# One decoder layer on one core: the first 512 channels projected together, in four banks, while x arrives

## The chip, the core and the metric

The kernel runs on one core of one Trainium2 chip. The metric is the device time of one execution in microseconds (us). The engines are named as the profile names them: PE is the matrix engine (PEld its weight loads), ACT the scalar engine, DVE the vector engine, POOL the general one, and SP the one that issues DMAs.

## What is computed

One layer of a decoder for 256 tokens of 1024 channels, all in float32: a combined projection of x, three branches that read it (block attention, a short convolution, dilated attention), their gated sum, an output projection and a layer norm, and then a gated feed-forward part with a convolution and a second layer norm. Cut to what matters:

```python
qa, ka, va, qd, kd, vd, b_gate, c_gate, hc, gate_logits = split(x @ w_in)   # x: 256 x 1024
y_moba = moba_attention(qa, ka, va)                    # 8 heads of 64
y_conv = b_gate * causal_dwconv(c_gate * hc, w_short_conv)
y_dil  = dilated_mixture(qd, kd, vd)                   # 12 heads of 64, 3 groups
g = sigmoid(gate_logits)
x = LN(alpha * x + (g0 * (y_moba @ w_moba_proj) + g1 * (y_conv @ w_conv_proj)
                    + g2 * (y_dil @ w_dil_proj)) @ w_mix_out)
u = causal_dwconv(x @ w_up, w_ffn_conv) + b_ffn_conv
x = LN(alpha * x + (silu(u_gate) * u_val) @ w_down)
```

## The kernel before, in words

All weights pass through SBUF once, as a stream of blocks of 1 MB: 1024 rows of a weight matrix by 256 columns. `load_next` (line 111) issues the DMA of a block on SP's queue into one of three `raw` buffers. `prep` (line 129) cuts a block into four pieces of 512 columns of the buffer and splits each into two float32r parts: ACT copies the piece rounded (`split`, line 149), DVE subtracts to get the remainder (line 150). Whoever splits the last piece of a block issues the load of the third next block. `LEAD = 10` bounds how many pieces may be split and not yet used.

A product of two split operands takes three matmuls, high by high, high by low and low by high. `project` (line 209) makes two tiles of 128 channels by 256 tokens: 48 matmuls of 256 columns, in one PSUM bank of the pool `acc` (three banks) for each tile. After each tile `tick` (line 155) splits the next pieces and runs the tile's consumer. For the queries of the dilated attention the consumer (`queries`, line 233) is two copies of 64 partitions by 256 columns on ACT (line 239), each followed by a subtraction on DVE (line 240).

The start differs from the steady course. Seven bf16 matmuls on zeros (`WARM`, line 172) stand first on PE. x comes in four quarters of 256 columns (256 KB), each followed on SP's queue by a quarter of the first weight block, then a quarter each of the second block, then the third block whole. PE transposes each quarter of x (four transposes, line 194) and ACT and DVE split it. `first_products` (line 94) makes the first two tiles of queries quarter by quarter: 12 matmuls (line 439) for each quarter, 48 in all. From line 112 on `project` makes the other tiles. In the tables below a "product" is one of these matmuls of 256 columns.

The order on each engine is fixed when the program is built: every engine takes its instructions strictly in its own list's order, and waits on semaphores for the others. Two rows of the layer norm's gain and offset (`gB`, `bB`, line 115) and small convolution weights (`small_loads`, line 411) are loaded on SP's queue too; the small weights are transposed on PE (lines 423 and 425).

Of the kernel before, what the change touches and what calls it, by code (L numbers as in the profile page):

```python
# [14 lines left out]
P = 128  # L15
# [18 lines left out]
WARM = 7  # L34
# [3 lines left out]
def trunk(ctx: ExitStack, tc, x, w_in, w_short_conv, w_moba_proj, w_dil_proj, w_conv_proj, w_mix_out,  # L38
# [27 lines left out]
    # ---- the stream of weights: blocks of up to [128, 2048] are loaded, and in pieces of 512 columns  # L66
    # ---- rounded to the tensor engine's 12-bit form, with the remainder
    blocks = []

    def block(*parts):  # L70
        """parts: DRAM access patterns [128, k, columns], one behind the other in the block"""
        blocks.append(parts)
# [10 lines left out]
    columns(DIL_Q, 3)  # L83
# [27 lines left out]
    def load_next(between=None):  # L111
# [5 lines left out]
        for p in blocks[i]:  # L117
            k, c = p.shape[1:]
            step = 2 if i < 2 else k
            for k0 in range(0, k, step):  # L120
                if between:
                    between(k0 // step)
                n = step * c
                nc.sync.dma_start(r[:, at:at + n].rearrange("p (k c) -> p k c", c=c), p[:, k0:k0 + step, :])  # L124
                at += n
# [3 lines left out]
    def prep(n=1):  # L129
        """the next n pieces, as far as they may run ahead"""  # L130
# [11 lines left out]
    def take(n):  # L142
        """the next n pieces"""
        i = used[0]
        assert len(ready) >= i + n, (len(ready), i, n)
        return ready[i:i + n]
# [5 lines left out]
    # ---- work set between the products that hold the tensor engine  # L152
    side, late = [], []

    def tick(n, consume=None, ahead=1):
        """after n pieces' worth of products: what the last time left, more weights, what takes these
        products, and a stage of the work that is set between"""
# [9 lines left out]
    # ---- the tensor engine's clock is raised while the first loads are under way  # L167
# [6 lines left out]
    # ---- x, and its transpose  # L174
    xs = act.tile([P, 2, D], F32, tag="xs", name="xs", bufs=2)
    xv = x.rearrange("(t p) c -> p t c", p=P)
    load_next(lambda c: nc.sync.dma_start(xs[:, :, c * 256:c * 256 + 256], xv[:, :, c * 256:c * 256 + 256]))  # L177
    for i in range(1, RAW):
        load_next()
# [17 lines left out]
    # ---- products  # L197
    def mm3(o, ah, al, bh, bl, first, last):
        """o += (ah + al)' (bh + bl), all but the product of the two remainders (2^-24)"""
# [4 lines left out]
    def cut(w, k, c0, c1):  # L204
        """rows k, columns c0..c1 of a block of 256 columns in pieces w"""
# [3 lines left out]
    def project(consume, xh=xTh, xl=xTl, ahead=1):  # L209
        """[128 channels, 256 tokens] for two tiles of channels; consume(tile, product)"""  # L210
# [7 lines left out]
    def project_tokens():  # L218
        """tokens by 256 channels, in two parts: [128 tokens, 2, 256 channels]"""
# [10 lines left out]
    # ---- attention: heads go in pairs, head a of a pair at partitions 64 a  # L230
    HALF = (slice(0, 64), slice(64, 128))

    def queries(store):
        """per tile of two heads: [part and remainder of a head, 2 heads, 256 tokens]"""
# [9 lines left out]
    def keys(store):  # L244
        """per tile: the part of a head, twice [128, 2 heads, 256 tokens]; the remainders [128, 256]"""
# [15 lines left out]
    def scores(o, q, k, a, t):  # L261
        """o [128 queries of tile t, 256 keys] for head a of a pair"""
# [5 lines left out]
    def exponentials(e, parts):  # L268
        """parts: (part of e, scores in PSUM, mask); e = exp((s + mask) / 8 - max); returns its sums"""
# [12 lines left out]
    def turned(blks):  # L282
        """transposes of up to four [128, 128] tiles, split: two of [128, 4, 128]"""
# [12 lines left out]
    def values(vs, ps, c):  # L296
        """vs: per group (vh, vl); ps: per group the transposed probabilities of keys 0..127 and 128..255"""
# [14 lines left out]
    def dilated(c, dq, dk, dv, y):  # L312
        """the stages of a pair of heads, the three groups in one softmax"""
# [75 lines left out]
    # ---- masks (additive), by shape alone  # L389
# [14 lines left out]
    # ---- small per-channel weights, turned to columns  # L404
# [24 lines left out]
    # ---- the mixer's projections and attention  # L429
    dq, dk, dv = [[], [], []], [[], [], []], []  # L430
    o = [acc((P, T)) for _ in range(2)]

    def first_products(k2):
        w = ready[k2]
        for xt, i in ((xTh, 0), (xTl, 0), (xTh, 1)):
            for k in (2 * k2, 2 * k2 + 1):
                for c in range(2):
                    s = (k % 2) * 256 + c * P
                    nc.tensor.matmul(o[c], w[i][:, s:s + P], xt[:, k, :], start=k + i == 0 and xt is xTh,  # L439
                                     stop=k == KT - 1 and i == 1)  # L440

    for k2 in range(KT // 2):
        transpose_x(k2)
        prep()
# [3 lines left out]
    q = queries(dq[0])  # L448
    for c in range(2):
        tick(2, lambda: q(c, o[c]), 1)  # L450
    for g in range(1, 3):
        project(queries(dq[g]), ahead=0)
    small_loads()
    gB, bB = rows(ln1_g, "gB"), rows(ln1_b, "bB")
# [48 lines left out]
    # ---- gates and branch projections  # L503
# [27 lines left out]
    # ---- layer norm  # L531
# [3 lines left out]
    def residual(r, res, o, st, i, c0, c1):  # L535
        """columns c0..c1 of r = ALPHA res + o, with their statistics"""
# [3 lines left out]
    def norm(r, st, gB, bB, ends, done=lambda c0, c1: None):  # L540
        """over r, in parts of columns that end at ends; done(first column, last)"""
# [12 lines left out]
    def row_products(o, a, w, k, t, c0, c1, first, last):  # L554
        """o += columns c0..c1 of row k of a block of 1024 columns, in pieces w, by the tokens of tile t"""
# [4 lines left out]
    def sums():  # L560
        """banks of the sums of the two token tiles by parts of the columns: (first column, last, sum)"""
# [5 lines left out]
    def finish(o, t, parts, r, res, between=lambda: None):  # L567
        """the last products of token tile t, in parts of columns that end one after the other, and the
        residual sum; parts: (activations, pieces of the weights)"""
# [14 lines left out]
    # ---- output projection of the mixer, tokens by channels  # L584
# [39 lines left out]
    # ---- gated feed-forward with a causal convolution  # L624
# [6 lines left out]
    def hidden(j):  # L631
        """the consumers of the two halves of w_up, and what they give"""
# [99 lines left out]
```

## Time and profile before

| | |
|---|---|
| times of three executions | 495.58, 497.87, 500.51 us, median 497.87 |
| span of the profiled execution, first to last instruction | 493.7 us |
| its own time | not given apart from its span; the span is 1.9 us under the shortest and 4.2 under the median of the three times |
| PE / PEld / DVE / ACT busy | 98% / 93% / 73% / 55% of the span |
| DMA | 83.51 MB, mean 169 GB/s |
| mean granted clock of PE | 0.991 |

The profile names a group of instructions by line, engine, operation and tiles (out<-in), with its busy time. A row of the timeline has start, length, engine, line, operation, tiles, shape and count; in brackets stands the idle time of the engine before it, and what ended it. A merged row's length runs from the first start to the last end; a matmul's own length is longer than the spacing to the next, since they are pipelined.

### The profile page before, as it was taken

The page shows a single profiled execution, that of the slowest core. Times are in us where ns is not written, and L with a number is a line of the kernel's source. Part 1 is how long each engine was busy: PE and PEld are TensorE (multiplying, and loading weights), DVE is VectorE, ACT ScalarE, POOL GpSimd, SP SyncE. Part 2 cuts the span into 40 slices and gives each one's busy share as a digit, 9 for nine tenths or more (in the row PEclk, how much of TensorE's full clock was granted, in tenths as well). Part 3 has the DMA queues.
Part 4 walks back from the last instruction along what each step waited for, and adds up shares of the span by engine and source line. Part 5 has one row for each costly group of instructions (what it writes and reads, how often), then busy time and mean ns, then how long its engine had stood idle before and what let it go on. Part 6 is the DMA issues. An engine that isn't in the chain of part 4 may idle for free.

```text
span 493.7 us, 9076 instructions
## 1 busy us (share of the span) xinstructions
PE 483.7 (98%) x3582; PEld 457.3 (93%) x3582; DVE 361.6 (73%) x775; ACT 271.9 (55%) x579; POOL 4.3 (1%) x9
## 2 busy tenths in 40 slices
PE   8999999999999999999999999999999999999993
PEld 5999788999899999999999889999999999999983
DVE  6888768476788865656565986798677867776966
ACT  4768455364756673535353712876655646565710
POOL 0000000000000000000000000000000000000000
PEclk9999899999999999999999999999999999999997
DMA  8975535353435163737374843546656374556102
GB/s 265 362 233 175 167 96 161 86 170 106 152 110 169 39 217 108 242 122 244 119 254 174 276 151 129 214 157 212 229 175 216 124 251 173 166 178 195 61 1 86
DMA packets 69502, 83.51 MB, mean 169 GB/s; under 512 B 1688, under 2 KB 64852, under 8 KB 69460
## 3 DMA queue, kind: packets, MB, share of 16 engines
q1 hardware_dynamic: 69460, 82.94, 51.4%
q8 instruction: 28, 0.46, 0.4%
q14 instruction: 14, 0.11, 0.1%
HBM read 81.89 MB, written 1.05 MB: 168 GB/s over the span
## 4 chain that ended last, share of the span: by engine, by line
PE 97%; DMA 1%; DVE 1%; SPq 0%; ACT 0%; issue 0%; DVEq 0%
PE acc L200 23%; PE acc L202 23%; PE acc L201 23%; PE att L200 6%; PE att L201 6%; PE att L202 6%; PE att L266 3%; PE att L265 2%; PE att L287 1%; PE acc L439 1%; DMA xs<-in_x_dram 1%; PE att L194 0%; DVE r L551 0%; SPq L124 0%; SPq L177 0%
## 5 line engine op out<-in xcount | busy, mean ns | idle before, releaser
L150 DVE TENSOR_TENSOR b<-raw,b 128x512 fp32r<-128x512 f32 x300 | 196.4, 686 | 39.6 <-ACT b L149 36.5
L149 ACT CAST b<-raw 128x512 fp32r<-128x512 f32 x300 | 169.6, 620 | 6.9 <-DMA raw<-in_w_in_dram 3.9
L200 PE MATMUL acc<-xTh,b 128*128 128x256 f32 x432 | 123.3, 285 | 0.0
L201 PE MATMUL acc<-xTl,b 128*128 128x256 f32 x432 | 122.2, 283 | 0.0
L202 PE MATMUL acc<-xTh,b 128*128 128x256 f32 x432 | 122.2, 283 | 0.0
L200 PE MATMUL acc<-x1Th,b 128*128 128x256 f32 x320 | 90.9, 284 | 0.0
L202 PE MATMUL acc<-x1Th,b 128*128 128x256 f32 x320 | 90.6, 283 | 0.0
L201 PE MATMUL acc<-x1Tl,b 128*128 128x256 f32 x320 | 90.5, 283 | 0.0
L200 PEld LDWEIGHTS acc<-xTh,b 128*128 128x128 f32 x432 | 82.8, 192 | 0.7
L201 PEld LDWEIGHTS acc<-xTl,b 128*128 128x128 f32 x432 | 82.8, 192 | 0.0
L202 PEld LDWEIGHTS acc<-xTh,b 128*128 128x128 f32 x432 | 82.8, 192 | 0.0
L201 PEld LDWEIGHTS acc<-x1Tl,b 128*128 128x128 f32 x320 | 61.4, 192 | 0.1
L200 PEld LDWEIGHTS acc<-x1Th,b 128*128 128x128 f32 x320 | 61.4, 192 | 0.1
L202 PEld LDWEIGHTS acc<-x1Th,b 128*128 128x128 f32 x320 | 61.4, 192 | 0.0
L629 DVE SCALAR_TENSOR_TENSOR b<-acc,fconv,b 128x255 f32<-128x255 f32 x80 | 38.4, 480 | 30.2 <-ACT b L627 29.2
L200 PE MATMUL att<-b,b 128*128 128x512 f32 (+1 forms) x170 | 58.9, 347 | 0.0
L201 PE MATMUL att<-b,b 128*128 128x512 f32 (+1 forms) x170 | 58.9, 347 | 0.0
L202 PE MATMUL att<-b,b 128*128 128x512 f32 (+1 forms) x170 | 58.7, 345 | 0.0
L149 ACT CAST b<-b 128x256 fp32r<-128x256 f32 x34 | 13.8, 408 | 47.3 <-DVE b L525 23.4
L627 ACT ACTIVATE b<-acc,fconv 128x256 f32<-128x256 f32 x40 | 22.6, 564 | 28.7 <-PE acc L202 28.6
L200 PEld LDWEIGHTS att<-b,b 128*128 128x128 f32 x170 | 32.2, 189 | 4.0
L202 PEld LDWEIGHTS att<-b,b 128*128 128x128 f32 x170 | 32.1, 189 | 4.0
(109 smaller groups left out, 646.6 us busy)
## 6 DMA issues: line engine op xcount, KB each, us to landing
raw<-in_w_in_dram SPq DMA_DIRECT2D x31, 1024.0 KB, 5.7
raw<-in_w_up_dram SPq DMA_DIRECT2D x22, 1024.0 KB, 5.1
raw<-in_w_down_dram SPq DMA_DIRECT2D x11, 1024.0 KB, 5.1
raw<-in_w_mix_out_dram SPq DMA_DIRECT2D x4, 1024.0 KB, 5.1
raw<-in_w_in_dram SPq DMA_DIRECT2D x8, 256.0 KB, 6.0
raw<-in_w_conv_proj_dram SPq DMA_DIRECT2D x4, 512.0 KB, 3.6
raw<-in_w_moba_proj_dram SPq DMA_DIRECT2D x4, 512.0 KB, 4.6
xs<-in_x_dram SPq DMA_DIRECT2D x4, 256.0 KB, 3.5
```

The costliest lines, as they stand in the source:

```text
L149: nc.scalar.copy(h, src)
L150: nc.vector.tensor_sub(l, src, h.bitcast(F32))
L200: nc.tensor.matmul(o, ah, bh, start=first, stop=False)
L201: nc.tensor.matmul(o, ah, bl, start=False, stop=False)
L202: nc.tensor.matmul(o, al, bh, start=False, stop=last)
L265: nc.tensor.matmul(o, q[:, a, ts], kd[:, a, :], start=True, stop=False)
L266: nc.tensor.matmul(o, q[HALF[a], a, ts], kl[HALF[a], :], start=False, stop=True)
L287: nc.tensor.transpose(p[:, i, :], b, ident)
L439: nc.tensor.matmul(o[c], w[i][:, s:s + P], xt[:, k, :], start=k + i == 0 and xt is xTh, stop=k == KT - 1 and i == 1)
L627: nc.scalar.activation(v, o, AF.Identity, bias=w[3], scale=w[0])
L629: nc.vector.scalar_tensor_tensor(v[:, j:], o[:, :T - j], w[j], v[:, j:], op0=OP.mult, op1=OP.add)
```

## The change

The first two blocks become 512 channels wide and half as deep (four pieces of 128 rows by 512 columns each); the first 512 channels, which are the first four tiles of queries, are accumulated together, two in banks of the pool `acc` and two in banks of `att`, with 24 matmuls for each quarter of x. The first two quarters of x are set before the two halves of the first block, the other two before the halves of the second; the third block comes in quarters. The consumers of all four tiles are called before the next pieces are split. `WARM` goes from 7 to 10, and the call that loads the layer norm's rows is written further down.

```diff
-WARM = 7
+WARM = 10
...
-    columns(DIL_Q, 3)
+    for k in (0, 4):
+        block(kview(w_in, DIL_Q, DIL_Q + 512, k, k + 4))
+    columns(DIL_Q + 512, 1)
...
-            step = 2 if i < 2 else k
+            step = 2 if i < 3 else k
             for k0 in range(0, k, step):
                 if between:
-                    between(k0 // step)
+                    between(at // 1024)
...
-    load_next(lambda c: nc.sync.dma_start(xs[:, :, c * 256:c * 256 + 256], xv[:, :, c * 256:c * 256 + 256]))
-    for i in range(1, RAW):
+
+    def load_x(c):
+        nc.sync.dma_start(xs[:, :, c * 256:c * 256 + 256], xv[:, :, c * 256:c * 256 + 256])
+
+    load_next(load_x)
+    load_next(lambda c: load_x(2 + c))
+    for i in range(2, RAW):
         load_next()
...
-    o = [acc((P, T)) for _ in range(2)]
+    o = [(acc if c < 2 else att)((P, T)) for c in range(4)]
 
     def first_products(k2):
-        w = ready[k2]
-        for xt, i in ((xTh, 0), (xTl, 0), (xTh, 1)):
-            for k in (2 * k2, 2 * k2 + 1):
-                for c in range(2):
-                    s = (k % 2) * 256 + c * P
-                    nc.tensor.matmul(o[c], w[i][:, s:s + P], xt[:, k, :], start=k + i == 0 and xt is xTh,
+
+        for k in (2 * k2, 2 * k2 + 1):
+            w = ready[k]
+            for xt, i in ((xTh, 0), (xTl, 0), (xTh, 1)):
+                for c in range(4):
+                    nc.tensor.matmul(o[c], w[i][:, c * P:c * P + P], xt[:, k, :], start=k + i == 0 and xt is xTh,
                                      stop=k == KT - 1 and i == 1)
 
     for k2 in range(KT // 2):
         transpose_x(k2)
-        prep()
+        prep(2)
         if k2:
             first_products(k2 - 1)
     first_products(KT // 2 - 1)
-    q = queries(dq[0])
-    for c in range(2):
-        tick(2, lambda: q(c, o[c]), 1)
-    for g in range(1, 3):
+    for g in range(2):
+        q = queries(dq[g])
+        for c in range(2):
+            q(c, o[2 * g + c])
+    tick(8)
+    for g in range(2, 3):
         project(queries(dq[g]), ahead=0)
     small_loads()
-    gB, bB = rows(ln1_g, "gB"), rows(ln1_b, "bB")
     side += [lambda: None, small_weights]
...
+    gB, bB = rows(ln1_g, "gB"), rows(ln1_b, "bB")
```

How the lists of the engines change is seen best in three places. In the rows `raw`, `b`, `acc` and `att` are buffers with their numbers; a DMAHW semaphore stands for a transfer's landing, Activation for ACT.

**PE, the start of the products.** Before, from the first transposes of x (`att<-ident,xs`) on:

```order
L194 MATMUL att_127<-ident,xs 128x128 [waits DMAHW2_49]
L194 MATMUL att_127<-ident,xs 128x128 x3
L194 MATMUL att_150<-ident,xs 128x128 [waits DMAHW4_49]
L194 MATMUL att_150<-ident,xs 128x128 x3
L439 MATMUL acc_114<-xTh,b_123 128x256 [waits Activation_49]
```

and with the change:

```order
L201 MATMUL att_135<-ident,xs 128x128 [waits DMAHW2_49]
L201 MATMUL att_135<-ident,xs 128x128 x3
L446 MATMUL acc_116<-xTh,b_127 128x256 [waits Activation_49]
L446 MATMUL acc_117<-xTh,b_127 128x256
L446 MATMUL att_118<-xTh,b_127 128x256
L446 MATMUL att_119<-xTh,b_127 128x256
L201 MATMUL att_176<-ident,xs 128x128 [waits DMAHW4_49]
L201 MATMUL att_176<-ident,xs 128x128 x3
L446 MATMUL acc_116<-xTl,b_127 128x256 [waits DVE_49]
```

Before, the transposes of the third quarter of x stand ahead of all products; now four products stand ahead of them, and the other 92 behind.

**ACT, behind the first products.** Before, with `acc_114` and `acc_115` the first two tiles of queries:

```order
L149 CAST b_218<-raw_84 128x512 [waits DMAHW2_49]
L239 CAST b_222<-acc_114 64x256 [waits PE_49]
L149 CAST b_227<-raw_84 128x512 [waits DMAHW3_49]
L239 CAST b_222<-acc_114 64x256 [waits DVE_49]
L149 CAST b_233<-raw_89 128x512 [waits DMAHW4_49]
```

and with the change, where `b_300` is the first piece of the block that PE takes next:

```order
L246 CAST b_280<-acc_116 64x256 [waits PE_49]
L246 CAST b_285<-acc_117 64x256 [waits PE_49]
L246 CAST b_290<-att_118 64x256 [waits PE_49]
L246 CAST b_295<-att_119 64x256 [waits PE_49]
L246 CAST b_280<-acc_116 64x256 [waits DVE_49]
L246 CAST b_285<-acc_117 64x256 [waits DVE_49]
L151 CAST b_300<-raw_88 128x512 [waits DMAHW0_49]
L246 CAST b_290<-att_118 64x256 [waits DVE_49]
L246 CAST b_295<-att_119 64x256 [waits DVE_49]
L151 CAST b_304<-raw_88 128x512 [waits DMAHW1_49]
```

Before, three of the next block's four pieces (`raw_84`) are copied ahead of the first wait for the tiles; now six copies of the tiles stand ahead of its first piece. PE, at the same place, now has:

```order
L446 MATMUL att_119<-xTh,b_227 128x256
L207 MATMUL acc_340<-xTh,b_300 128x256 [waits Activation_49]
L208 MATMUL acc_340<-xTl,b_300 128x256
L207 MATMUL acc_378<-xTh,b_300 128x256 [waits DVE_49,PE_49]
L208 MATMUL acc_378<-xTl,b_300 128x256
L209 MATMUL acc_340<-xTh,b_301 128x256 [waits DVE_49]
```

The first product of the third stretch of channels follows the last of the first stage directly, and the fifth needs the remainder `b_301` from DVE.

**SP's queue.** With the change, from behind the third block on:

```order
L416 DMA gB_2298<-in_ln_g_dram 128x1024 [waits DMAHW4_49]
L126 DMA raw_150<-in_w_in_dram 128x8x256 [waits DMAHW5_49,DVE_49]
L126 DMA raw_230<-in_w_in_dram 128x8x256 [waits DMAHW7_49,DMAHW6_49,DVE_49]
L416 DMA bB_2300<-in_ln_b_dram 128x1024
L126 DMA raw_316<-in_w_in_dram 128x8x256 [waits DMAHW2_49,DMAHW1_49,DMAHW3_49,DMAHW0_49,DVE_49]
L126 DMA raw_334<-in_w_in_dram 128x8x256 [waits DMAHW5_49,DVE_49]
L126 DMA raw_407<-in_w_in_dram 128x8x256 [waits DMAHW6_49,DVE_49]
L422 DMA b_114<-in_w_short_conv_dram 12x128
```

Before, `gB` stands at the same place, `bB` one block earlier, and the small weights one block earlier. On PE the small weights' transposes now stand behind the third tile of keys, before they stood behind the second.

## Rows read from the trace of the kernel before

**Rows 1.** From the page: the span; busy time, share and count of each engine; shares of the chain that ended last, by engine.

```profile
span 493.7 us, 9076 instructions
PE 483.7 (98%) x3582; PEld 457.3 (93%) x3582; DVE 361.6 (73%) x775; ACT 271.9 (55%) x579; POOL 4.3 (1%) x9
...
PE 97%; DMA 1%; DVE 1%; SPq 0%; ACT 0%; issue 0%; DVEq 0%
```

**Rows 2.** The chain that ended last, in order of time, its start: start us, length us, what.

```profile
2.75 4.78 DMA xs<-in_x_dram
7.57 1.11 PE att L194 x4
8.68 0.85 PE acc L439 x4
```

**Rows 3.** The timeline of PE over the first 16 us.

```profile
1.19 3.17 PE L172 MATMUL acc<-warm 128*128 128x512 bf16 x7 [1.19 <-DVE warm L169]
4.15 1.06 PE L194 MATMUL att<-ident,xs 128*128 128x128 f32 x4
6.02 1.11 PE L194 MATMUL att<-ident,xs 128*128 128x128 f32 x4 [0.81 <-DMA xs<-in_x_dram]
7.57 1.11 PE L194 MATMUL att<-ident,xs 128*128 128x128 f32 x4 [0.43 <-DMA xs<-in_x_dram]
...
8.69 0.84 PE L439 MATMUL acc<-xTh,b 128*128 128x256 f32 x3
9.33 0.63 PE L194 MATMUL att<-ident,xs 128*128 128x128 f32 x2
9.61 1.09 PE L439 MATMUL acc<-xTl,b 128*128 128x256 f32 x4
10.55 1.11 PE L439 MATMUL acc<-xTh,b 128*128 128x256 f32 x8
11.50 0.64 PE L439 MATMUL acc<-xTl,b 128*128 128x256 f32 x4
...
12.46 0.38 PE L194 MATMUL att<-ident,xs 128*128 128x128 f32 x2
12.60 0.72 PE L439 MATMUL acc<-xTh,b 128*128 128x256 f32 x4
13.15 0.64 PE L439 MATMUL acc<-xTl,b 128*128 128x256 f32 x4
...
15.06 0.64 PE L439 MATMUL acc<-xTh,b 128*128 128x256 f32 x4
15.54 0.28 PE L200 MATMUL acc<-xTh,b 128*128 128x256 f32 x1
```

**Rows 4.** Busy time of each engine in stretches at both ends of the span, with counts, the granted clock, the DMA share and the bytes moved (GB/s, last column).

```profile
2.00:4.00 2.00, 2.00 (x6) 0.84 (x5) 1.17 (x5) 0.02 (x1) 0.00 (x0) 1.00 0.94 280
4.00:6.00 2.00, 1.21 (x5) 0.66 (x3) 0.40 (x1) 1.05 (x2) 0.00 (x0) 1.00 0.91 258
6.00:8.00 2.00, 1.55 (x6) 1.15 (x7) 1.11 (x3) 0.89 (x3) 0.00 (x0) 1.00 1.01 321
8.00:10.00 2.00, 2.00 (x12) 2.00 (x11) 1.74 (x4) 1.48 (x4) 0.00 (x0) 1.00 1.04 344
10.00:12.00 2.00, 2.00 (x17) 2.00 (x17) 1.94 (x4) 1.14 (x2) 0.00 (x0) 1.00 1.09 364
...
486.00:488.00 2.00, 0.25 (x3) 0.05 (x1) 1.61 (x5) 0.00 (x0) 0.23 (x1) 1.00 0.00 0
```

**Rows 5.** The timeline of ACT and DVE where the first weights land, and behind the first products.

```profile
4.95 0.62 ACT L149 CAST b<-raw 128x512 fp32r<-128x512 f32 x1 [2.94 <-DMA raw<-in_w_in_dram]
...
15.62 0.37 ACT L239 CAST b<-acc 64x256 fp32r<-64x256 f32 x1 [1.12 <-PE acc L439]
15.89 0.62 ACT L149 CAST b<-raw 128x512 fp32r<-128x512 f32 x1
...
16.02 0.42 DVE L240 TENSOR_TENSOR b<-acc,b 64x256 fp32r<-64x256 f32 x1 [0.64 <-ACT b L239]
16.55 0.69 DVE L150 TENSOR_TENSOR b<-raw,b 128x512 fp32r<-128x512 f32 x1
...
18.37 1.14 ACT L149 CAST b<-raw 128x512 fp32r<-128x512 f32 x2
19.53 0.77 ACT L239 CAST b<-acc 64x256 fp32r<-64x256 f32 x2
```

**Rows 6.** The same columns as rows 4, in the stretch of the first attention scores.

```profile
46.00:48.00 2.00, 2.00 (x19) 2.00 (x19) 1.96 (x5) 1.97 (x5) 0.00 (x0) 1.00 0.51 171
48.00:50.00 2.00, 2.00 (x10) 1.23 (x8) 1.94 (x4) 1.54 (x4) 0.00 (x0) 1.00 0.34 46
50.00:52.00 2.00, 2.00 (x7) 1.13 (x7) 1.97 (x8) 0.81 (x1) 0.00 (x0) 0.85 1.03 366
52.00:54.00 2.00, 2.00 (x10) 2.00 (x10) 1.79 (x5) 1.33 (x5) 0.00 (x0) 0.50 0.35 113
54.00:56.00 2.00, 2.00 (x16) 2.00 (x15) 0.00 (x0) 0.00 (x0) 0.00 (x0) 0.80 0.43 65
56.00:58.00 2.00, 2.00 (x10) 1.22 (x9) 1.07 (x3) 0.89 (x2) 0.00 (x0) 1.00 1.04 366
```

**Rows 7.** The timeline of SP's queue: issues of the layer norm's rows and of the small weights; and PE, where it takes the small weights.

```profile
8.25 1.81 SPq L409 DMA_DIRECT2D gB<-in_ln_g_dram  x1
...
25.70 0.59 SPq L415 DMA_DIRECT2D b<-in_w_short_conv_dram  x1
26.35 1.14 SPq L417 DMA_DIRECT2D b<-in_w_ffn_conv_dram  x3
27.53 0.35 SPq L418 DMA_DIRECT2D b<-in_b_ffn_conv_dram  x1
...
33.08 0.23 PE L423 MATMUL att<-ident,b 12*128 12x12 f32 x1
```

## The prediction

> **What bounds the kernel now.** I read the page first, then the chain of waits, then the timeline of the first 16 us. The page says that PE is busy for 483.7 of 493.7 us, and 97% of the chain that ended last is PE [rows 1]. So there are 10 us in which PE does nothing, and they lie at the two ends: behind 486 us only the last layer norm runs, with PE busy 0.25 us of two [rows 4], which is about 7.5 us; the other 2.4 us or so are waits before 8 us. In between, products follow each other every 0.12 us (the four from 15.06 on take until 15.54) [rows 3]. Since PE is the bound everywhere behind the start, a microsecond gained or lost in the start comes through to the end unchanged, and nothing behind it can give it back: there is no later wait worth naming.
>
> The start hangs on x. The chain begins with the third quarter of x, which lands at 7.57 us, then its transposes, then products [rows 2]. PE waits 0.81 and 0.43 us for quarters [rows 3]. PE also runs at half clock there: three products from 8.69 to 9.33 stand 0.21 us apart, from 10.55 on 0.12 us. The page's granted clock of 1.00 [rows 4] does not show this first low stretch; the spacing does. 48 products are done at 15.54 us, and 96 would be at 15.54 + 48 x 0.12 = 21.3 us. That is what the change must beat.
>
> **The change, part by part.**
>
> *Arrival and the first 96 products.* On PE the transposes of x's third quarter stand ahead of 92 of the 96 products. Up to and with that quarter the queue carried 5 x 0.262 = 1.31 MB, which landed by 7.57 us; now the two halves of the first block are twice as large, and it is 3 x 0.262 + 2 x 0.524 = 1.84 MB. The added 0.52 MB at 321 to 344 GB/s [rows 4] take 1.6 us, so the quarter lands at about 9.15 us. Four transposes at 0.21 us follow (three spacings and one length make the 1.06 us of four [rows 3]), to 10.0. Then 92 products at 0.12 us are 11.05 us, and the four transposes of the last quarter, which stand among them, 0.1 us each (two transposes and four products from 12.46 to 13.15 [rows 3]): 21.45 us. If the clock rises at 10.5 us as before, the products ahead of that cost 0.25 us more: 21.7. If it is up before the third quarter, the transposes cost 0.4 instead of 0.85 us: 21.0. I take 21.4, which is **+0.1 us** against 21.3, with bounds of -0.3 and +0.4.
>
> *The ten warming matmuls* stand 3.17 / 7, nearly 0.43 us, apart [rows 3], so three more end at 5.5 us instead of 4.2, and x's first transposes with them. Their cover: the first product needs the first half block, which lands a good microsecond after the 4.95 us of the first quarter now [rows 5], needs a 0.62 us copy, and stands behind the second quarter's transposes, which land with 0.26 MB more ahead of them, at 6.8. Cost nothing; without that cover it would be 1.3 us. Whether ten raise the clock sooner is open: before, PE worked from 1.19 to 5.2 almost without a break, and the transposes at 7.57 were still slow. I put it into the bounds above.
>
> *The consumers ahead of the next pieces.* This is the largest term. Let E be the moment at which PE could start the next product. The first bank's last product is the fourth from the end: issued at E - 0.48, 0.28 us long, and ACT starts 0.04 us behind its end, at E - 0.16 (before, the first bank's last product was issued at 15.06 + 2 x 0.12 = 15.30, ended at 15.58, and ACT started at 15.62 [rows 3, 5]). ACT then has six copies of 64x256 in its list ahead of the first piece of the next block; one and the copy behind it start 0.27 us apart [rows 5], so 1.62 us, and the piece's copy runs from E + 1.46 to E + 2.1. PE stands for **2.1 us**, which nothing covers: its next instruction needs this piece. Four products follow, to E + 2.6. The fifth needs the remainder, which DVE makes behind seven subtractions on the tiles; the last of those ahead of it needs the copy that ACT makes behind the piece (two 128x512 copies take 1.14, so start 0.52 apart: E + 1.98 to 2.35), takes to about E + 2.75, and the remainder 0.69 us [rows 5]: E + 3.5. PE stands **0.9 us** more. Afterwards pieces come every 0.6 us and are used every 0.72. Sum **+3.0 us**. Bounds: copies at 0.385 us apart (two took 0.77, the second with a wait [rows 5]) give 3.7; if the last subtraction ahead of the remainder is not in the way, 2.5. In the kernel before three of four pieces were split while the products ran, so none of this existed.
>
> *The clock in this stall.* Of the 3.5 us behind E PE works 0.5. In the stretch of the first scores it issued 17 matmuls in 4 us, fewer than half the usual 19 for each 2 us, and its granted clock went to 0.85, 0.50 and 0.80 in three stretches of 2 us, 0.3 + 1.0 + 0.4 = 1.7 us lost; ten in 56 to 58 us brought no fall [rows 6]. The stall is emptier than both, so I expect a fall in most executions. Part of the low stretch would lie on the stall itself: **+1.2 us** (0 to 1.7). The Trainium skill (TensorE: Matmul & The Clock Gate, "Why this matters for your kernels") ties falls in mid-kernel to gaps in which the engine is idle; the trace is harsher, since the fall of rows 6 came with PE busy 2.00 of 2.00 us. [...]
>
> *Moves on SP's queue.* The gain row of the layer norm still stands directly behind the third block, so that edit moves nothing where it matters; the offset row goes one block later and is not needed by any product. Small weights are issued one block later and used one tile (2.9 us) later. Before, they were issued until 27.9 us and used at 33.08 [rows 7]; now their issue waits until eleven more pieces at 0.6 us are split behind the stall, at E + 10, about 32 us, ends at 35, and PE asks for them 48 products, the stall and three tiles of 2.9 us behind E, at E + 17.5, near 39 us. That is 4 us instead of 5, behind two blocks. I cost it at nothing; uncovered it would be up to 1 us.
>
> *The sum:* 0.1 + 3.0 + 1.2 = +4.3 us; the span of 493.7 goes to 498.0. The profiled execution's full time is not given; its span lies 4.2 us under the median of 497.87, and I carry the difference to the median: **502.2 us**, +0.9%. About 1%, 5 us, is what a measurement of this kernel can tell from no change.
>
> **Rivals.**
>
> 1. *The stall without the fall of the clock.* For it: 10 and 8 matmuls for 2 us did not always bring one [rows 6]. 501.0 us. Chance 0.25.
>
> 2. *The clock rises late.* At about 8.2 us PE has done its four products and waits for the third quarter until 9.15; before, it worked on from 7.57 until the clock rose near 10.5 [rows 3]. If that break puts the rise off by as long a low stretch as rows 6 show, 1.7 us are lost. It decides if the products behind 10.5 us still stand 0.21 us apart. 502.2 - 0.3 + 1.7 = 503.6. Against it: ten warming matmuls and the first transposes are 5 us of work without a break. 0.12.
>
> 3. *Not slower: fewer falls elsewhere.* The three times spread over 4.9 us, three times the 1.7 us of one fall. If the scores' stretch loses two falls against the median execution before, 502.2 - 3.4 = 498.8. It decides if the clock stays at 1.00 through the scores. Against it: their instructions do not change. 0.11.
>
> 4. *The loads come faster.* The first 6 us ran at 258 to 321 GB/s, from 10 us on at 364 [rows 4]. At 364 from 2 us on, the 1.84 MB, and 0.27 MB of later loads that are always under way by then (1.58 MB moved by 7.57 against 1.31), land at 7.8 us, 1.3 sooner: 500.9. The Trainium skill (DMA: Bandwidth & Descriptors, "Specifications") gives a limit of about 358 GB/s for HBM for each core; the trace agrees from 8 us on (344 and 364), not ahead of it, and by that figure alone this rival would be the rule. 0.07.
>
> 5. *The order on the chip makes less of the stall,* so that the first stage's full banks win. Nothing in the rows speaks for it, except that PE would then gain up to 1.3 us by the arrival of rival 4: at best 496.6. 0.03.
>
> **How the numbers follow.** The forecast has 0.42; its own range, by the bounds of its terms, is 500.5 to 504. The range for 8 in 10 runs from 498.8, which rival 3 gives, to 504.2, which takes in rival 2 and the upper bounds. Slower by over 1% begins at 502.85: about 0.4 of the forecast (0.17), rival 2 (0.12) and the upper end of rival 1 (0.04) make 0.33. Faster by over 1% would need 492.9: 0.03. Within 1%: 0.64.
>
> **What would show it.** Right: the third quarter of x at about 9.1 us, the 96th product near 21.4; behind it PE idle for about 2 us, ended by ACT's copy of a piece, and again for about 0.9, ended by DVE; the granted clock at 0.5 somewhere in 24 to 29 us; from there on the same rows some 4 us later. Wrong: no such idle time behind the first products, or an end of the first 96 products well ahead of 20 us, or later waits on PE that are not in this trace.

## The result and the profile after

The changed kernel takes 502.66 us (median of 18 executions, 498.57 to 505.16), the kernel before on the same chip 497.70 (18 executions, 494.00 to 501.75). The ratio is 1.0112, 95% interval 1.0081 to 1.0142: slower by about 1%, 5 us. The ratios here and below are those on record; they leave out the one execution that counts as slow (503.93 us, with two pieces ahead) and are not always the quotient of the two medians.

The profiled execution took 503.57 us, its span is 501.8. The page of the changed kernel, the lines that answer to [rows 1]: span; busy time of the two PE rows; granted clock in 40 slices; shares of the chain of waits.

```profile
span 501.8 us, 9078 instructions
PE 487.8 (97%) x3585; PEld 460.4 (92%) x3585; DVE 360.8 (72%) x775; ACT 271.5 (54%) x579; POOL 4.3 (1%) x9
...
PEclk9989978999999999999999999999999999999997
...
PE 94%; DVE 2%; DMA 1%; ACT 1%; issue 1%; SPq 0%; DVEq 0%; ACTq 0%
```

ACT and DVE have come into the chain with 3% where they had one. The third digit of the clock (25 to 38 us) and the sixth and seventh (63 to 88 us) are below 9: low clock behind the first products, and again in the stretch of the scores. (The granted clock is the share of PE's full clock; in the rows it has two levels, 1.00 and 0.50, and a stretch that has both shows their mean.)

The timeline of PE in the changed kernel (start us, length us, what, times; in brackets the idle time before and what ended it), beside [rows 3]. New line numbers: 174 warming, 201 transposes of x, 446 the first 96 products, 207 to 209 the products of `project`.

```profile
1.19 4.18 PE L174 MATMUL acc<-warm 128*128 128x512 bf16 x10 [1.19 <-DVE warm L171]
5.20 0.60 PE L201 MATMUL att<-ident,xs 128*128 128x128 f32 x4
6.66 0.66 PE L201 MATMUL att<-ident,xs 128*128 128x128 f32 x4 [0.86 <-DMA xs<-in_x_dram]
8.92 0.66 PE L201 MATMUL att<-ident,xs 128*128 128x128 f32 x4 [1.08 <-DMA xs<-in_x_dram]
...
20.64 0.40 PE L446 MATMUL att<-xTh,b 128*128 128x256 f32 x2
23.25 0.39 PE L207 MATMUL acc<-xTh,b 128*128 128x256 f32 x1 [2.22 <-ACT b L151]
23.48 0.28 PE L208 MATMUL acc<-xTl,b 128*128 128x256 f32 x1
...
23.72 0.28 PE L208 MATMUL acc<-xTl,b 128*128 128x256 f32 x1
24.83 0.39 PE L209 MATMUL acc<-xTh,b 128*128 128x256 f32 x1 [0.83 <-DVE b L152]
```

And the timeline of PE in the kernel before, the product behind the 96th and the first product of the keys, the 145th; behind them the 145th in the changed kernel:

```profile
21.40 0.36 PE L200 MATMUL acc<-xTh,b 128*128 128x256 f32 x1
...
27.23 0.28 PE L200 MATMUL acc<-xTh,b 128*128 128x256 f32 x1
```

```profile
31.68 0.28 PE L207 MATMUL acc<-xTh,b 128*128 128x256 f32 x1
```

The 96th product is issued at 20.76 us, so PE could go on at 20.88, half a microsecond sooner than the kernel before, whose next product behind the 96th starts at 21.40. Then PE stands until 23.25 (2.37 us), does four products, and stands again until 24.83 (0.99 us beyond the spacing of 0.12).

What ACT and DVE do in that time, by the timelines of ACT and of DVE in the changed kernel:

```profile
20.72 0.64 ACT L246 CAST b<-acc 64x256 fp32r<-64x256 f32 x2 [4.81 <-PE acc L446]
21.25 0.64 ACT L246 CAST b<-att 64x256 fp32r<-64x256 f32 x2
21.92 0.64 ACT L246 CAST b<-acc 64x256 fp32r<-64x256 f32 x2
22.58 0.62 ACT L151 CAST b<-raw 128x512 fp32r<-128x512 f32 x1
```

```profile
23.12 0.94 DVE L247 TENSOR_TENSOR b<-att,b 64x256 fp32r<-64x256 f32 x2
24.08 0.69 DVE L152 TENSOR_TENSOR b<-raw,b 128x512 fp32r<-128x512 f32 x1
```

ACT works through six copies of the finished queries (line 246) and only then takes the piece that PE needs (line 151). DVE makes the remainder of that piece (line 152) behind its subtractions (line 247). Both ends fit PE's two starts.

Busy times in stretches of 2 us in the changed kernel (columns as in [rows 4]: PE, PEld, DVE, ACT, POOL, granted clock, DMA share, GB/s):

```profile
22.00:24.00 2.00, 0.74 (x4) 0.54 (x4) 1.76 (x5) 1.93 (x6) 0.00 (x0) 1.00 0.50 194
24.00:26.00 2.00, 1.17 (x8) 1.17 (x8) 1.91 (x5) 2.00 (x4) 0.00 (x0) 0.86 0.02 8
26.00:28.00 2.00, 2.00 (x11) 2.00 (x11) 2.00 (x4) 2.00 (x5) 0.00 (x0) 0.50 0.00 0
28.00:30.00 2.00, 2.00 (x16) 2.00 (x15) 2.00 (x4) 1.67 (x5) 0.00 (x0) 0.79 0.66 175
```

The clock went to its lower level at 25.4 us, behind the stall, and cost 0.28 + 1.00 + 0.42 = 1.7 us of the three stretches, about 1.5 of it on the path. The first product of the keys, the 145th, starts at 31.68 us; before, at 27.23. That is 4.45 us. A further 0.6 us is lost near 44 and 51 us, where PE waits for banks (below), but 0.3 of it comes back: if the time from the keys to the last matmul is taken without half of its low time, it is 457.6 us after and 457.3 before. Together 4.75 us, where the medians differ by 4.96. The two profiled spans differ by more, 8.1 us, because this execution had more low stretches among the scores (at 63 to 70 and 76 to 80 us, 10.2 us in all) than the one of before, which had one of 3.4 us [rows 6]; half of the 6.8 us is 3.4.

The mean granted clock of every execution of the changed kernel is on record as well. Its median over the 18 is 0.984; for the kernel before it was 0.987 in the three later comparisons (79 executions; those of this comparison have none on record). One low stretch of 3.4 us takes 1.7 us of some 500, or 0.0034, off the mean. That fits one such stretch more in the median execution, the one in the stall. It is not an exact count, since the mean also holds the low stretch behind the last matmul, 2.1 to 5.4 us long in the profiles, which costs no time.

### The profile page after: what moved, and what is told of

It is laid out like the page before. It is cut to its first block, busy times and chain, and to the rows that moved or that the text cites. A ratio compares the mean times of both kernels' runs of the same rounds, so it can differ in the third digit from the quotient of the medians.

```text
span 501.8 us, 9078 instructions
## 1 busy us (share of the span) xinstructions
PE 487.8 (97%) x3585; PEld 460.4 (92%) x3585; DVE 360.8 (72%) x775; ACT 271.5 (54%) x579; POOL 4.3 (1%) x9
## 4 chain that ended last, share of the span: by engine, by line
PE 94%; DVE 2%; DMA 1%; ACT 1%; issue 1%; SPq 0%; DVEq 0%; ACTq 0%
PE acc L207 22%; PE acc L209 22%; PE acc L208 22%; PE att L207 6%; PE att L208 6%; PE att L209 6%; PE att L273 2%; PE att L272 2%; PE att L294 1%; DMA xs<-in_x_dram 1%; PE acc L446 1%; PE att L446 1%; ACT b L246 0%; DVE b L152 0%; DVE b L264 0%
## 5 line engine op out<-in xcount | busy, mean ns | idle before, releaser
L207 PE MATMUL acc<-xTh,b 128*128 128x256 f32 x416 | 119.6, 288 | 2.4 <-ACT b L151 2.2
L209 PE MATMUL acc<-xTh,b 128*128 128x256 f32 x416 | 118.2, 285 | 0.8 <-DVE b L152 0.8
L208 PE MATMUL acc<-xTl,b 128*128 128x256 f32 x416 | 118.3, 284 | 0.0
L207 PEld LDWEIGHTS acc<-xTh,b 128*128 128x128 f32 x416 | 80.4, 193 | 3.3 <-ACT b L151 2.4
L209 PEld LDWEIGHTS acc<-xTh,b 128*128 128x128 f32 x416 | 80.4, 193 | 1.0 <-DVE b L152 1.0
L208 PEld LDWEIGHTS acc<-xTl,b 128*128 128x128 f32 x416 | 80.5, 194 | 0.0
```

The lines of the kernel that those rows point to most:

```text
L207: nc.tensor.matmul(o, ah, bh, start=first, stop=False)
L208: nc.tensor.matmul(o, ah, bl, start=False, stop=False)
L209: nc.tensor.matmul(o, al, bh, start=False, stop=last)
```

## The experiments

Each is compared with the kernel before on the same chip. The moment of the first product of the keys is used throughout: 27.23 us before, 31.68 after.

**The pieces split ahead of the consumers.** The theory on trial: the stall exists because the next weights' splitting stands behind the consumers in ACT's and DVE's lists.

```diff
     first_products(KT // 2 - 1)
+    used[0] += 8
+    prep(4)
     for g in range(2):
         q = queries(dq[g])
...
-    tick(8)
+    prep(5)
```

> The changed kernel with the next block's four pieces split ahead of the consumers of the first four tiles. Theory (the list's order makes a stall of about 3.4 us, and the clock falls in it for another 1.5): PE goes from the 96th product into the third stretch without a wait, no fall of the clock between 20 and 30 us, the first product of the keys at 26.5 to 27 us instead of 31.7, time 4 to 5 us under the changed kernel, about equal to the kernel before (ratio 0.998 to 1.003). Rival (the wide blocks or the four banks themselves cost the time, through arrival or PSUM): the waits behind the 96th product go, but the time stays within 1.5 us of the changed kernel (ratio 1.008 to 1.012). Rival (later falls of the clock are the loss): keys start early, but the time stays over 1.005.

Measured: 499.64 us, ratio 1.0022 (0.9991 to 1.0052). The stall is gone: the product behind the 96th starts at 21.13 us, the clock does not fall between 20 and 30, and the keys start at 26.89, 4.8 us sooner. But a new wait came in. Its rows are these, first the waits of PE from 3 to 56 us in this kernel (line waiting, line waited for: us in total, times, longest us):

```profile
PE att L201 <- DMA xs<-in_x_dram: 2.0, 2, 1.1
PE acc L207 <- DVE b L247: 1.7, 1, 1.7
PE acc L207 <- DVE b L264: 0.2, 1, 0.2
```

And DVE's timeline there:

```profile
25.52 3.70 DVE L152 TENSOR_TENSOR b<-raw,b 128x512 fp32r<-128x512 f32 x6
29.25 0.42 DVE L247 TENSOR_TENSOR b<-acc,b 64x256 fp32r<-64x256 f32 x1
29.70 1.29 DVE L152 TENSOR_TENSOR b<-raw,b 128x512 fp32r<-128x512 f32 x2
31.02 0.88 DVE L247 TENSOR_TENSOR b<-acc,b 64x256 fp32r<-64x256 f32 x2
```

Six remainders stand ahead of the first subtraction that reads the third stretch's bank, and two more ahead of the second, which empties it. With only three `acc` banks PE waits for that, 1.67 us until 31.60. The stall's cause is shown, and also that splitting too much ahead moves it. The sooner keys are not kept: the first product of the values, the 289th, starts at 48.57 us, 3.35 later than before (45.22). That the total is only 0.2% longer goes with a higher clock than before, 0.9905 in the median against 0.987; why these executions fell less often among the scores is not shown.

**Two pieces ahead instead of five.** As the kernel above, but `prep(2)` in place of `prep(5)`.

> e1 with two pieces instead of five split behind the consumers of the first tiles. In e1 the stall behind the 96th product went, but PE waited 1.7 us at 29.8 us for a bank whose consumer stands in DVE's list behind seven pieces split ahead. Theory (each of these waits is the list's order and nothing else): no wait of PE over 0.3 us from 20 to 35 us, the keys begin at 26.5 to 27 us and their second stretch at 32.3 to 32.8 (before: 27.2 and 33.1; e1: 26.9 and 34.5); ratio 0.997 to 1.002. Rival (the bank comes free late for another reason): the second stretch begins after 34 us.

Measured: 498.62 us, ratio 1.0012 (0.9975 to 1.0050). PE works without a break over the whole place where the changed kernel stood; the keys start at 26.62 us, 0.6 sooner than before. Behind them a wait is left, though. The timeline of PE in this kernel, where it takes the small weights and at the first product of the values, and the latter in the kernel before:

```profile
32.85 0.23 PE L430 MATMUL att<-ident,b 12*128 12x12 f32 x1 [0.21 <-DMA b<-in_w_short_conv_dram]
...
46.12 0.28 PE L207 MATMUL acc<-b,xTh 128*128 128x256 f32 x1
```

```profile
45.22 0.28 PE L200 MATMUL acc<-b,xTh 128*128 128x256 f32 x1
```

The five transposes of the small weights, which before stood together (33.08 to 33.45 us), now lie spread from 32.85 to 35.99, the first of them behind a wait for its load; the second stretch of the keys starts at 33.00, where 32.8 at the latest had been expected, and the values 0.9 us later than before. So the kernel without the stall takes as long as the kernel before, and the 0.6 us that it gains in the start are lost again there.

**The stall filled with work.** Twenty products that are thrown away (into the bank that the next stretch starts anew) stand on PE where it would be idle; ACT's and DVE's lists stay. This separates the wait from the clock.

```diff
-            o = acc((P, T))
+            o = fill.pop() if fill else acc((P, T))
...
+    fill.append(acc((P, T)))
+    for i in range(20):
+        nc.tensor.matmul(fill[0], ready[7][1][:, 0:P], xTh[:, 7, :], start=True, stop=True)
     for g in range(2, 3):
         project(queries(dq[g]), ahead=0)
```

> The changed kernel with 20 extra products in the stall behind the 96th product: they go into the bank that the third stretch starts anew, so what is computed does not change. They take 20 x 0.12 = 2.4 us, as long as the first wait. Theory (the clock falls because the stall is empty, and that is a cost of its own): the waits of ACT and DVE end at the same time as before, no fall at 24 to 29 us, the keys start 1.3 to 1.7 us sooner than 31.7 us, ratio 1.007 to 1.009. Rival (the fall has nothing to do with the stall, or costs nothing since PE waits anyway): the keys start at 31.5 us or later, ratio 1.011 or more.

Measured: 499.69 us, ratio 1.0049 (1.0017 to 1.0081). PE's timeline in this kernel, and its stretches:

```profile
20.97 2.56 PE L464 MATMUL acc<-xTh,b 128*128 128x256 f32 x20
23.36 0.36 PE L207 MATMUL acc<-xTh,b 128*128 128x256 f32 x1
...
24.92 0.39 PE L209 MATMUL acc<-xTh,b 128*128 128x256 f32 x1 [0.84 <-DVE b L152]
```

```profile
24.00:26.00 2.00, 1.16 (x10) 1.08 (x9) 1.91 (x5) 1.98 (x5) 0.00 (x0) 1.00 0.01 4
26.00:28.00 2.00, 2.00 (x19) 1.95 (x18) 2.00 (x5) 2.00 (x5) 0.00 (x0) 1.00 0.00 0
```

The first real product starts as late as in the changed kernel (23.36 against 23.25), the second wait stays, but the clock does not fall, and the keys start at 30.39 instead of 31.68. So the fall came from the idle time, and its price in the start is 1.3 us. The total came down by more than that, and by more than was expected (1.0112 to 1.0049, some 3 us). The rest goes with the granted clock on record: its median over these executions is 0.9925 against 0.984, of which the one fall in the stall is 0.0034, so that there was less low clock later on too. Why is not shown.

**Small weights requested sooner.** The call `small_loads()` stands ahead of `tick(8)`, all else as changed. It tests whether the waits near 44 and 51 us hang on the small weights.

> The changed kernel with the loads of the small convolution weights called ahead of the third stretch, so that they stand one block earlier on SP's queue and their transposes behind the second tile of keys again. Theory (DVE waits for these transposes in its list, holds up the keys' consumers and with them a bank that PE needs): DVE's wait of 2.6 us ahead of the copy of these weights and PE's two waits near 45 and 51 us, together 0.6 us, go; the stall and the fall behind the 96th product stay; ratio 1.009 to 1.011. Rival (those waits have another cause): PE still waits 0.5 us or more between 42 and 52 us.

Measured: 502.68 us, ratio 1.0098 (1.0062 to 1.0133). The two waits are gone: two of the five transposes of the small weights now lie where PE would stand in the stall (at 24.05 and 24.25 us), the other three at 37.4, and between the keys' start and 49 us no product is issued more than 0.22 us behind the instruction ahead of it, where the changed kernel has two gaps of 0.446 and 0.435. The first wait of the stall and the fall at 25.0 us stay. In the total the 0.6 us do not show; the interval is wider than that.

**Seven warming matmuls in the changed kernel.** `WARM = 7` instead of 10.

> The changed kernel with 7 warming matmuls instead of 10. Theory (ten raise the clock sooner, but the first products wait for x anyway): the transposes at the third quarter stand 0.21 instead of 0.11 us apart, the 96th product ends 0.3 to 0.7 us later than 20.9 us, the stall behind it stays 3.4 us; time within 1 us of the changed kernel, ratio 1.010 to 1.014 to the kernel before. Rival (three more matmuls delay the start): the 96th product ends up to 1.3 us sooner, ratio about 1.008.

Measured: 503.40 us (4 executions), ratio 1.0120 (1.0071 to 1.0169). The 96th product is issued at 23.49, 2.7 us later than with ten; 0.3 to 0.7 had been expected. PE's timeline and stretches:

```profile
7.06 0.66 PE L201 MATMUL att<-ident,xs 128*128 128x128 f32 x4 [2.12 <-DMA xs<-in_x_dram]
```

```profile
8.00:10.00 2.00, 1.19 (x6) 0.89 (x6) 2.00 (x5) 1.55 (x3) 0.00 (x0) 0.50 1.06 393
10.00:12.00 2.00, 2.00 (x11) 2.00 (x10) 1.52 (x4) 1.14 (x2) 0.00 (x0) 0.50 1.07 374
```

The clock rose at 4.5 us, fell again at 7.95, behind a wait of 2.12 us for x, and stayed low until 14.8. The sign of rival 2 of the prediction shows here (products still 0.21 us apart behind 10.5 us), but the break is another: rival 2 had the wait for the third quarter of x, and here the clock fell ahead of that, behind the wait for the second. The two gaps of the stall are the same (2.49 and 1.12 us between issues). The total does not show the 2.7 us: this execution had 3.4 us of low clock among the scores where that with ten had 10.2.

**x sooner.** In the changed kernel the order of SP's loads becomes x0, w, x1, x2, w, x3, w, w (w: half blocks), since PE's list needs x2 before the second half block.

```diff
-    load_next(load_x)
-    load_next(lambda c: load_x(2 + c))
+    load_next(lambda c: [load_x(i) for i in ((0,), (1, 2))[c]])
+    load_next(lambda c: load_x(3) if c == 0 else None)
```

> The changed kernel with the third quarter of x set ahead of the second half of the first block on SP's queue, and the fourth ahead of the second block. Theory (92 of the 96 products hang on the third quarter, and 0.52 MB fewer ahead of it land it 1.4 us sooner): its transposes at 7.4 to 8.0 us instead of 8.9, the 96th product issued at 19.4 to 20.0 us instead of 20.8, the stall behind it unchanged at 3.4 us; ratio 1.007 to 1.011. Rival (the second half block becomes what PE waits for): PE waits between 9 and 12 us, and the 96th product stays at 20.4 us or later.

Measured: 501.42 us (4 executions), ratio 1.0101 (1.0060 to 1.0142). The third quarter's transposes start at 7.77 instead of 8.92 us, the 96th product at 19.56, the keys at 30.49: 1.2 us sooner right through. The stall is unchanged and the clock falls at 24.0. In the total, with four executions, the interval is too wide to tell the 1.2 us.

**Ten warming matmuls in the kernel before.** `WARM = 10` there, nothing else.

> The kernel before with 10 warming matmuls instead of 7 and nothing else. Theory (ten raise the clock before the first products, which then run at 0.12 instead of 0.21 us): the granted clock rises by 7 us instead of 10.5, the 48th product ends 0.5 to 1.2 us sooner than 15.5 us; ratio 0.996 to 1.000. Rival (the clock falls again while PE waits for x, or three matmuls put off the start): the 48th product at 15.5 us or later, ratio 1.000 to 1.004.

Measured: 499.00 us, ratio 1.0035 (1.0003 to 1.0067): a miss, it is not faster. The clock did rise sooner, at 6.8 instead of 10.45 us, but the product behind the 48th starts only 0.2 sooner (15.34), where 0.5 to 1.2 had been expected. And the lists built for the engines came out otherwise: the offset row `bB` (512 KB) is now issued ahead of the next block, ACT stands 2.37 us for that block, and PE 0.70 us for a bank:

```profile
25.00 0.36 PE L200 MATMUL acc<-xTh,b 128*128 128x256 f32 x1 [0.70 <-DVE b L240]
```

**x sooner in the kernel before.** The order x0, w, x1, x2, w, x3, w, w there, with quarter blocks.

> The kernel before with the third quarter of x set ahead of the second quarter of the first block on SP's queue, and the fourth behind it; nothing else. Theory (before the change too the start hangs on the third quarter, 0.26 MB sooner is 0.8 us; wide first blocks are worth something beyond that, since 24 products for each quarter cover the loads): the quarter's transposes at 6.7 to 7.2 us, the 48th product ends 0.3 to 0.9 us sooner than 15.5; ratio 0.997 to 1.001, above the 0.994 of e6. Rival (the sooner x is all that e6 gained, and the narrow blocks would do as well): ratio 0.993 to 0.996.

Measured: 496.95 us, ratio 0.9988 (0.9947 to 1.0028). The product behind the 48th starts at 13.93 us, 1.6 sooner than before, where 0.3 to 0.9 had been expected, that behind the 96th at 20.04 instead of 21.40, and the keys at 25.86; but in the time this is not told from no change. Part of it is the clock, which rose at 5.13 us in this execution and at 10.45 in that of the kernel before; how much is x alone is not shown.

**All three repairs together.** The changed kernel with the pieces split ahead (4, then 2), x in the order above, and `small_loads()` ahead of `prep(2)`.

> The first 512 channels together as in the change, with pieces split ahead of the consumers and two behind them (e7), the third quarter of x sooner (e8) and the small weights loaded early (e5). Theory (the start is a sum of such waits): the 96th product issued at 19.4 to 20.0 us, the keys at 25.5 to 26.2, their second stretch at 31.3 to 32, 1.2 to 1.7 us ahead of the kernel before, no waits at 44 and 50 us; ratio 0.994 to 0.999. Rival (the time is set by how often the clock falls later on, whatever the start): ratio 1.000 or more although the keys begin sooner.

Measured: 493.47 us (12 executions, 492.12 to 497.78), ratio 0.9939 (0.9911 to 0.9968): it beats the kernel before, 497.38 in the same comparison, and with it the changed one. The page and PE's timeline of this kernel:

```profile
span 490.4 us, 9077 instructions
...
PEclk9999999999999999999999999999999999999999
```

```profile
7.74 0.60 PE L201 MATMUL att<-ident,xs 128*128 128x128 f32 x4
...
19.40 0.40 PE L446 MATMUL att<-xTh,b 128*128 128x256 f32 x2
19.64 0.28 PE L207 MATMUL acc<-xTh,b 128*128 128x256 f32 x1
```

The view of waits lists none on PE between 3 and 56 us. The keys start at 25.40, 1.8 us sooner than before; the transposes of the small weights stand together again (31.25 to 31.61), and the values start at 43.39, still 1.8 sooner. The rest of the 3.9 us between the medians goes with the clock: its median over these executions is 0.994, over those of the kernel before in the same comparison 0.987. At the same clock of 0.994 four executions of this kernel took 493.3 us on average and five of the kernel before 495.0, which is 1.7 us, as the start has it. Why there were fewer falls is not shown.

Nor is it shown that the wide blocks are needed for the 1.8 us: with narrow blocks and x sooner the keys started at 25.86 us, only 0.46 later than here, with the clock up at 5.13 us against 6.68, and the two ratios' intervals overlap.

**The same with seven warming matmuls.**

> e6 with 7 warming matmuls instead of 10. Theory (ten keep PE at work until x's first transposes, and the clock is up and stays up; with seven it fell at 8 us in e2 and the 96th product came 2.7 us later): the clock rises later than 7 us or falls once ahead of 15 us, the 96th product issued 0.3 to 2.7 us later than in e6 (19.5 us), ratio 0.995 to 1.000. Rival (the number of warming matmuls does not matter once nothing waits): 96th product within 0.3 us of e6, ratio 0.992 to 0.996.

Measured: 497.33 us, ratio 0.9977 (0.9935 to 1.0018). The first transposes and products run at the low clock until 10.5 us, 0.21 us apart:

```profile
6.80 1.11 PE L201 MATMUL att<-ident,xs 128*128 128x128 f32 x4 [1.59 <-DMA xs<-in_x_dram]
...
9.41 0.63 PE L446 MATMUL att<-xTl,b 128*128 128x256 f32 x2
...
10.62 0.40 PE L446 MATMUL acc<-xTh,b 128*128 128x256 f32 x2
```

The product behind the 96th starts at 21.33, 1.7 us later than with ten. So with x early the three warming matmuls were worth 1.7 us of the start between these two executions; with seven the clock does not always rise so late (last section). The total is not clearly told from that with ten (the intervals overlap), nor from that of the kernel before (its interval takes in 1).

## Why the prediction was right, and where its terms were off

It said 502.2 us; 502.66 was measured. The mechanism is the one that it named: a stall which the edit itself makes behind the 96th product. The first experiment shows its cause (with the lists' order turned round it is gone), the third that the fall of the clock is its consequence. That the sum met the median to half a microsecond is partly luck: by the trace the terms are -0.5, +3.4, +1.5 and +0.3, together 4.7 where 4.3 was forecast, and the start that came 0.6 us sooner than forecast made up for most of the 1.0 by which the three others came out dearer.

- **Arrival and the first 96 products: +0.1 predicted, -0.5 by the trace.** This lies just outside the bound of -0.3. The third quarter's transposes came at 8.92 instead of 9.15 us, and the clock was already up at 4.96 us (four transposes in 0.60 us where [rows 3] have 1.06). The bounds had allowed for the second, not for both together.
- **The ten warming matmuls: 0 predicted.** In the changed kernel itself they end at 5.4 us and hold up nothing on the path: the next wait is for x. Their gain, which the prediction left open, is the sooner rise of the clock; with seven the start was 2.7 us longer in the one execution that was profiled.
- **The stall: 3.0 predicted, 3.4 measured** (2.37 + 0.99). The copies' count and the order of the lists were right. The six copies took 1.86 us, 0.31 each (20.72 to 22.58), where the prediction had put 0.27; it lay within the bounds.
- **The fall of the clock: 1.2 predicted, about 1.5 by the trace, 1.3 by the run that filled the stall.** All four kernels that left the stall empty fell there in the profiled execution (the changed one, small weights sooner, seven warming matmuls, x sooner); none of the eight without the stall or with it filled did. So rival 1 did not come. It had also read the rows wrongly: the thin stretches of [rows 6] that kept the clock have ten matmuls, and the eight is a count of weight loads.
- **SP's queue: 0 predicted, 0.6 measured, of which 0.3 is left at the last matmul. This step failed.** The prediction asked whether the small weights would land in time, and they do: they are issued at 33.0 to 34.8 us, about where it put them. What it left out is the engine behind. Timelines of DVE and ACT, and of PE, in the changed kernel:

```profile
41.65 0.17 DVE L433 COPY sconv<-att 128x12 f32<-128x12 f32 x1 [2.63 <-PE att L432]
...
43.42 0.37 ACT L259 CAST b<-acc 64x256 fp32r<-64x256 f32 x1 [3.42 <-DVE b L264]
```

```profile
50.98 0.35 PE L207 MATMUL acc<-b,xTh 128*128 128x256 f32 x1 [0.16 <-DVE b L264]
```

PE transposes the small weights at 40.41 us (before at 33.08 [rows 7], 5.85 us behind the keys' start; now 8.7 behind it). DVE's next instruction is the copy of these transposes, and it waits 2.63 us for them with the keys' work behind it; ACT waits 3.42 us for DVE; and PE twice has to wait for a bank. Issues are 0.446 and 0.435 us apart there instead of 0.12, which is 0.6 us. Where the small weights are loaded sooner, the waits are gone.

The sentence that behind the start there is "no later wait worth naming" holds for the kernel before; the change itself made two. The gain row of the layer norm did move nothing (issued at 8.89, before at 8.25 [rows 7]).

- **Rival 2 (the clock rises late)** did not come in the changed kernel. With seven warming matmuls its sign came, through an earlier break than the prediction described (the wait for the second quarter) and as a fall behind an early rise; it cost 2.7 us, not 1.7. **Rival 3 (fewer falls)**: the changed kernel's profile has more of them, not fewer, and the median clock of its 18 executions is lower than that of the kernel before, not higher. **Rival 4 (faster loads)** came only in part: 308, 351 and 395 GB/s in the three stretches from 4 to 10 us, against 258, 321 and 344 [rows 4], and this brought the quarter 0.2 us forward, not 1.3. The Trainium skill (DMA: Bandwidth & Descriptors, "Specifications") puts the limit of HBM at about 358 GB/s for a core; the trace's mean from 8 to 20 us, 367, is near it, and its stretch of 2 us at 395 is above it, so here that figure is no hard ceiling. **Rival 5** did not come.

The prediction's own range has a slip: the lower bounds of its terms, -0.3 + 2.5 + 0, lead to 500.1 us and not to 500.5.

What stays open is why the clock falls more or less often among the scores. Over the profiles it was low there, from 50 to 90 us, for none to three times 3.4 us, in kernels whose work there is the same. Single executions of one kernel spread by it (those of the changed kernel have mean clocks from 0.978 to 0.994), and the kernels' medians differ by it as well (0.994 with all repairs, 0.987 with two pieces ahead), which no run here explains.

## What to carry to other kernels

When a first stage is made wider, its results come all at once; read in the lists of the other engines what then stands ahead of the next stage's operands, and put just enough of these operands ahead of the results: with none PE stood 3.4 us here, with four and then five pieces 1.7, with four and then two it did not stand at that place. An empty stretch on PE is to be priced twice, once as the wait and once as the low clock behind it. And moving an instruction to a later place in one list must be followed through every list in which others stand behind its results, even where its data come in good time.

## What was not expected of the hardware

Warming: in the eight kernels with ten warming matmuls PE's clock was up by 7.0 us at the latest (4.04 to 6.96). In the four with seven it rose at 10.45, 10.52, 5.13 and 4.53 us, and in the last one fell again while PE waited for x. With seven the start could go either way, with ten it did not in any profile taken here.

Low clock with a busy PE: in the changed kernel, as before [rows 6], the clock also fell where PE counts as busy without a pause, in stretches with seven to ten matmuls instead of 19:

```profile
62.00:64.00 2.00, 2.00 (x7) 1.16 (x6) 2.00 (x10) 0.36 (x2) 0.00 (x0) 0.75 0.50 173
64.00:66.00 2.00, 2.00 (x10) 2.00 (x10) 1.97 (x6) 1.92 (x5) 0.00 (x0) 0.50 0.00 0
```

Other stretches as thin (eight matmuls in 54 to 56 and in 60 to 62 us of the same execution) kept the clock.
